# Twelve instead of eight K tiles of the mLSTM's gates and values in seven products

## The chip, the cores and the metric

The kernel runs on one core of one Trainium2 chip. It is a program for TensorE (matrix products), VectorE (DVE), ScalarE (ACT), GpSimd (POOL) and SyncE (SP, which issues most of the loads). The metric is the time of one execution on the device in microseconds (us); the kernel before takes 2147.57 us, the median of three runs (2147.09 to 2148.02).

## The reference

Two layers of an encoder trunk on x of shape (1, 256, 2048), all in float32. Layer 0 mixes with pooling and grouped-query attention, layer 1 with a bidirectional mLSTM of 8 heads of 256 dimensions; each layer ends with a gated MLP of width 5632. The change lies in the mLSTM of layer 1, which is, cut to what matters:

```
proj = h @ w_in                       # 256 x 2048 by 2048 x (4*2048 + 32)
q, k, v = proj's first three blocks of 2048 columns, by heads; q *= 256 ** -0.5
o_gate  = sigmoid(proj's fourth block of 2048 columns)
gates   = proj's last 32 columns + b_gate        # input and forget gates, both directions
w       = exp(log weights from the gates, running-max stabilised, causal or anti-causal)
scores  = (q . k) * w
h_t     = (scores @ v) / max(|sum of scores|, exp(-m))    # forward, and backward on the flipped sequence
y       = rms_norm per head(h_fw + h_bw) * o_gate;   x = x + y @ w_out
```

## The kernel before, in words

All matrix products take float32 operands as a high and a low part (the tiles `hl` for weights, index 0 high, index 1 low), and every product is three matmuls: high by high, high by low, low by high. Activations stand transposed: `norm.xx[:, k]` is K tile k (128 of the 2048 channels) for 256 tokens.

**Weights.** They arrive as a stream of chunks of 128 x 1024 numbers (512 KB), in the order in which TensorE uses them. `Stream.load` (L117) issues a chunk's load on SP's queue into one of seven raw buffers `w`; `Stream.split` makes the high part on ACT (L137) and the low part on DVE (L138) into one of four buffers `hl`. A chunk that is a sum of others is prepared in one of two ways. As `Made` it is summed beforehand in DRAM by `premix` (L491): ACT's queue copies a part into a scratch `m`, and POOL's queue adds other parts to it with accumulating DMAs, each of them held until a chosen matmul has run ("paced"). As `Chain` the raw part is loaded, and DVE adds the sum that stands in the preceding chunk (L133 and L134, two additions of 128 x 512) ahead of the split.

**TensorE's order** is written out by hand. The main products call `wv.tick`, and a weave (`Weave`) of generators puts the small matmuls of the heads (`qk`, `atr`, `av`, `htr`) between them: a generator yields the number of us of main products to wait before its next step. The orders of ACT, DVE, POOL and SP are made by a planner from the dependencies and its own durations.

**The mLSTM layer** (L780) first makes values and the 32 gate columns for heads 0 and 1 (`mv`), and `gates` turns the gate columns into rows: `gr` goes to DRAM as `gd`, and each head reads two rows of it back, broadcast over 128 partitions, into `G` (L874). It then goes over four pairs of heads `hp`. For each head `stat_group` makes q and k (`mq`, `mk`, 16 K tiles each), `scaled` gathers them, multiplies by the tokens' norm factor (q also by 256 ** -0.5, L854) and splits them into `hl_q`, `hl_k`; `head` is added to the weave. For the first three pairs `gates_values` follows (tiles `mp`, `mo`, `mv`): the output gate's 512 columns of this pair, and the values' 512 columns of the next pair, in one pass over K.

**Seven products.** Over K tiles 0 to 7, that is four pairs of K tiles (`ML_PAIRS`), this pass takes two token blocks by two K tiles by two column blocks with seven products instead of eight. `ML_ORDER` is its order: an `A` takes four products of a pair from two chunks (summed weights, `Made` or `Chain`) and sums of activations (`comb`, made by `combine`), a `B` two products from one chunk, a `P` one product each of two pairs from one chunk. The other K tiles are taken directly: a `D` (gates) or an `E` (values) is four products of two K tiles from one chunk. `first` and `second` combine the partial sums from PSUM on ACT and DVE into `og` and `vf`.

## Time and profile before

| | us |
|---|---|
| median of the runs (lowest, highest) | 2147.57 (2147.09, 2148.02) |
| the profiled execution's own time | 2147.11 |
| its span | 2145.3 |
| busy: TensorE, weight load, DVE, ACT, POOL | 2139.5, 1834.6, 1784.1, 1444.6, 287.6 |
| mLSTM from its first product to the output projection | 965.1 to 1344 |
| `gates_values` of the three pairs | 1038.1 to 1084.3, 1133.2 to 1177.4, 1226.2 to 1271.4 |

The times of the trace count from the start of the span; PE is TensorE's matmuls, PEld its weight loads. A group of instructions is given as line, engine, operation, tile out<-in, count, busy time, mean of one in ns, and the idle time of the engine ahead of it with what ended that. A window is given as us, then busy time (and count) of PE, PEld, DVE, ACT and POOL, the granted TensorE clock, the busy share of the DMA engines and GB/s.

### The profile page before, as it was taken

How to read it: one execution, taken by the hardware profiler on the slowest of the kernel's cores; microseconds unless marked ns; L12 is line 12 of the kernel's file. 1: busy time of each engine (PE TensorE's matmuls, PEld its weight loads, DVE VectorE, ACT ScalarE, POOL GpSimd, SP SyncE). 2: the span in 40 equal slices, each digit the busy share in tenths (PEclk: the TensorE clock that was granted, in tenths of full speed). 3: DMA queues.
4: the chain of work that ended last, by engine and by line, in shares of the span. 5: the costliest groups of instructions: out<-in, count | busy, mean ns of one | idle time of the engine just before them, and what ended most of it. 6: DMA issues, size and time to landing. Idle time of an engine off the chain costs nothing.

```text
span 2145.3 us, 32359 instructions
## 1 busy us (share of the span) xinstructions
PE 2139.5 (100%) x11364; PEld 1834.6 (86%) x11364; DVE 1784.1 (83%) x2524; ACT 1444.6 (67%) x2199; POOL 287.6 (13%) x366
## 2 busy tenths in 40 slices
PE   9999999999999999999999999999999999999999
PEld 7888888888888888889888888888888888888887
DVE  7786678889988899898878786567888899889988
ACT  6665577777777767766556564557776777777774
POOL 0022112111111111111111111111111111100000
PEclk9999999999999999999999999999999999999999
DMA  9678889899999999998889798988999999888875
GB/s 333 210 213 256 262 248 317 275 327 329 318 331 320 321 300 306 307 296 237 276 276 299 232 308 236 280 242 247 313 291 333 337 311 317 288 259 266 255 249 189
DMA packets 181543, 606.66 MB, mean 283 GB/s; under 512 B 23707, under 2 KB 26563, under 8 KB 181379
## 3 DMA queue, kind: packets, MB, share of 16 engines
q1 hardware_dynamic: 133952, 478.60, 62.4%
q0 software_dynamic: 28384, 70.54, 19.4%
q10 hardware_dynamic: 19042, 55.45, 7.8%
q8 instruction: 89, 1.46, 0.3%
q14 instruction: 76, 0.61, 0.1%
HBM read 602.35 MB, written 104.90 MB: 330 GB/s over the span
## 4 chain that ended last, share of the span: by engine, by line
PE 97%; DVE 2%; issue 1%; DMA 0%; ACT 0%; ACTq 0%; DVEq 0%
PE up L275 45%; PE pp L275 16%; PE op L275 8%; PE mq L275 4%; PE mk L275 4%; PE mo L275 3%; PE mv L275 3%; PE qproj L275 3%; PE dn L275 3%; PE mp L275 1%; PE kproj L275 1%; PE vproj L275 1%; DVE hl L138 1%; PE pool L275 1%; PE av L275 1%
## 5 line engine op out<-in xcount | busy, mean ns | idle before, releaser
L138 DVE TENSOR_TENSOR hl<-w,hl 128x1024 fp32r<-128x1024 f32 (+1 forms) x869 | 1048.0, 1217 | 179.1 <-ACT hl L137 172.1
L137 ACT CAST hl<-w 128x1024 fp32r<-128x1024 f32 (+1 forms) x868 | 891.2, 1046 | 384.8 <-PE up L275 118.3
L275 PE MATMUL up<-xx,hl 128*128 128x512 f32 (+1 forms) x5632 | 993.6, 337 | 0.0
L275 PEld LDWEIGHTS up<-xx,hl 128*128 128x128 f32 x5632 | 867.0, 188 | 130.0
L491 POOL DMA_DIRECT2D m<-m x184 | 147.4, 816 | 942.9 <-PE up L275 414.0
L275 PE MATMUL pp<-hl,s 128*128 128x512 f32 x912 | 226.5, 390 | 0.4
L275 PEld LDWEIGHTS pp<-hl,s 128*128 128x128 f32 x912 | 168.1, 188 | 34.4 <-DVE hl L138 1.6
L275 PE MATMUL pp<-hl,g 128*128 128x512 f32 x684 | 173.9, 390 | 0.0
L275 PEld LDWEIGHTS pp<-hl,g 128*128 128x128 f32 x684 | 125.8, 188 | 24.4
L441 ACT COPY tb_up<-up 128x512 f32<-128x512 f32 x88 | 51.6, 587 | 116.5 <-PE up L275 116.5
L1122 DVE TENSOR_TENSOR y<-y,z 128x510 f32<-128x510 f32 x88 | 60.8, 690 | 63.2 <-ACT y L1121 62.7
L1121 ACT ACTIVATE y<-tb_up,conv 128x256 f32<-128x256 f32 x176 | 103.7, 589 | 0.0
L491 POOL DMA_DIRECT2D m<-in_dn x80 | 69.2, 864 | 247.1 <-PE up L275 59.4
L275 PE MATMUL mk<-xx,hl 128*128 128x512 f32 (+1 forms) x512 | 93.0, 338 | 0.0
L275 PE MATMUL mq<-xx,hl 128*128 128x512 f32 (+1 forms) x512 | 92.0, 337 | 0.0
L442 DVE TENSOR_TENSOR tb_up<-up,tb_up 128x512 f32<-128x512 f32 x88 | 60.9, 692 | 36.9 <-ACT tb_up L441 36.5
L275 PE MATMUL op<-hl,cat 128*128 128x512 f32 x384 | 91.5, 393 | 0.0
L1119 ACT ACTIVATE z<-tb_up,conv 128x256 f32<-128x256 f32 x176 | 88.2, 501 | 3.9 <-DVE tb_up L1114 2.0
L275 PE MATMUL op<-hl,mcat 128*128 128x512 f32 x384 | 89.7, 392 | 0.0
L275 PEld LDWEIGHTS mq<-xx,hl 128*128 128x128 f32 x512 | 79.2, 188 | 11.6
L275 PEld LDWEIGHTS mk<-xx,hl 128*128 128x128 f32 x512 | 79.3, 188 | 11.4
L1120 ACT ACTIVATE z<-tb_up,conv 128x256 f32<-128x256 f32 x176 | 87.4, 496 | 0.0
(256 smaller groups left out, 2178.8 us busy)
## 6 DMA issues: line engine op xcount, KB each, us to landing
w<-in_up SPq DMA_DIRECT2D x352, 512.0 KB, 6.6
w<-in_dn SPq DMA_DIRECT2D x174, 512.0 KB, 6.0
w<-in_m_in SPq DMA_DIRECT2D x118, 512.0 KB, 6.0
w<-m SPq DMA_DIRECT2D x98, 512.0 KB, 5.7
m<-in_dn ACTq DMA_DIRECT2D x160, 256.0 KB, 5.8
m<-m POOLq DMA_DIRECT2D x184, 128.0 KB, 6.0
w<-in_a_in SPq DMA_DIRECT2D x45, 512.0 KB, 5.5
m<-in_dn POOLq DMA_DIRECT2D x80, 256.0 KB, 7.2
```

Source lines behind the costliest of these rows:

```text
L137: (self.nc.vector.tensor_copy if i + c == 0 else self.nc.scalar.copy)(hl[:, 0, c : c + n], w[:, c : c + n])
L138: low = self.nc.vector.tensor_sub(hl[:, 1, c : c + n], w[:, c : c + n], hl[:, 0, c : c + n].bitcast(F32))
L275: last_mm[0] = pe.matmul(out_, lhsT, rhs, start=start, stop=stop, skip_group_check=True)
L441: a.copy(tb, ps[:, :, 1, :])
L442: v.tensor_add(tb, ps[:, :, 0, :], tb)
L491: paced(eng.dma_start(to[p : p + P // 2], src[p : p + P // 2], **kw))
L1119: a.activation(z[:, 0, j, :], u[:, j, :], AF.Copy, scale=cw(tl, 0))
L1120: a.activation(z[:, 1, j, :], u[:, j, :], AF.Copy, scale=cw(tl, 2))
L1121: a.activation(y[:, j, :], u[:, j, :], AF.Identity, scale=cw(tl, 1), bias=cw(tl, 3))
L1122: v.tensor_add(y[:, :, 1:S], y[:, :, 1:S], z[:, 0, :, 0 : S - 1])
```

## The change

1. `ML_PAIRS` goes from 4 to 6: K tiles 0 to 11 are taken by seven products, K tiles 12 to 15 directly. `ML_ORDER` becomes six A, two D, six B, two E and three P, with A4, A5 and B0 to B5 in a row, where before a D stood behind each A. The activations' sums of pairs 4 and 5 get a tile of their own in the layer's constants.
2. In the third pass (`hp == 2`) each pair's second A chunk is a `Chain`; in the others, as before, only that of odd pairs.
3. q is no longer multiplied in `scaled`; its norm factor and 256 ** -0.5 stand in `qrcol`, one number for each token, and go into the operation that multiplies the scores by their weights (L891) in place of a 1.0. `hl_q` has one buffer in place of two.
4. `G` of head 0 is loaded from POOL's queue; the other heads' from ACT's.
5. The gaps of `head`: 14.0 and 9.0 for 10.0 and 6.0 ahead of `atr`, 5.0 for 3.2 ahead of `av`.
6. The premix of layer 1's MLP begins after the second pass instead of the first, one sum each 28.0 instead of 30.0; that of the mLSTM begins two up-projections later in layer 0's MLP, one sum each 18.0 instead of 25.0, and makes 18 sums instead of 12.

```diff
-ML_PAIRS = 4
-ML_ORDER = [(e[0], int(e[1:] or 0)) for e in "A0 D A1 D A2 D A3 D B0 B1 B2 E B3 E P0 E P2 E".split()]
+ML_PAIRS = 6
+ML_ORDER = [(e[0], int(e[1:] or 0)) for e in "A0 A1 D A2 A3 D A4 A5 B0 B1 B2 B3 B4 B5 E P0 P2 E P4".split()]
...
-            comb = actp.tile([P, ML_PAIRS, 2, 4, P], F32R, tag="B1", name="mcomb")
+            combs = [actp.tile([P, 4, 2, 4, P], F32R, tag="B1", name="mcomb0")]
+            combs.append(kp.tile([P, ML_PAIRS - 4, 2, 4, P], F32R, tag="mcomb", name="mcomb1"))
...
-            def scaled(ps, name, scale):
+            def scaled(ps, name):
                 u = gather(tp, ps, name)
-                v.scalar_tensor_tensor(u, u, scale, bc(norm.R, 2), ALU.mult, ALU.mult)
-                r = tp.tile([P, 2, 2, S], F32R, tag=name[0] + "hl", name=f"hl_{name}")
+                if name[0] == "k":
+                    v.tensor_mul(u, u, bc(norm.R, 2))
+                r = tp.tile([P, 2, 2, S], F32R, tag=name[0] + "hl", bufs=2 - (name[0] == "q"), name=f"hl_{name}")
...
-                    a.dma_start(G[:, d, :], gd[r : r + 1, :].to_broadcast([P, S]))
+                    (g if h == 0 else a).dma_start(G[:, d, :], gd[r : r + 1, :].to_broadcast([P, S]))
...
-                    v.scalar_tensor_tensor(arg[:, o : o + n], qk[:, t, c : c + n], 1.0, arg[:, o : o + n],
+                    v.scalar_tensor_tensor(arg[:, o : o + n], qk[:, t, c : c + n], qrcol[:, t : t + 1], arg[:, o : o + n],
...
-                yield 10.0 if h % 2 else 6.0
+                yield 14.0 if h % 2 else 9.0
...
-                yield 3.2
+                yield 5.0
...
+                    qrcol = kp.tile([P, 2], F32, tag="qrcol", name="qrcol")
+                    v.tensor_scalar_mul(qrcol, norm.rcol, MD ** -0.5)
...
-                hp == 0 and premix(1, 30.0, 30.0, 0)
+                hp == 1 and premix(1, 28.0, 28.0, 0)
...
-                    if layer == 0 and (c, i) == (len(FCH) - 2, 5):
-                        premix(2, 25.0, 25.0, 0)
+                    if layer == 0 and (c, i) == (len(FCH) - 2, 7):
+                        premix(2, 18.0, 18.0, 0)
...
-            made = [Made()] if j % 2 else [Made(), Made()]
+            made = [Made()] if j % 2 or hp == 2 else [Made(), Made()]
             part = [p[hp * ML_PAIRS + j] for p in parts]
             mixes.append(part + [made])
-            out += made + [Chain(part[2])] * (j % 2)
+            out += made + [Chain(part[2])] * (2 - len(made))
```

More of the change, by code (lines that the diff above doesn't have):

```diff
@@ L961, in combine @@
                 v.tensor_sub(sf[:, 3], g4[:, 2], sf[:, 2])
-                a.copy(comb[:, j, 0], sf)
-                v.tensor_sub(comb[:, j, 1], sf, comb[:, j, 0].bitcast(F32))
+                a.copy(comb(j)[:, 0], sf)
+                v.tensor_sub(comb(j)[:, 1], sf, comb(j)[:, 0].bitcast(F32))
             def combos():
@@ L1028, in gates_values @@
                     if kind == "A":
-                        xs = [[comb[:, j][:, i, m] for i in range(2)] for m in (1, 0, 2)] + [x_part(2 * j + 1, 1)]
+                        xs = [[comb(j)[:, i, m] for i in range(2)] for m in (1, 0, 2)] + [x_part(2 * j + 1, 1)]
                     elif kind == "B":
@@ L1032, in gates_values @@
                     elif kind == "P":
-                        xs = [[comb[:, j + k][:, i, 3] for i in range(2)] for k in range(2)]
+                        xs = [[comb(j + k)[:, i, 3] for i in range(2)] for k in range(2)]
                     else:
@@ L1072, in mlstm_layer @@
                     v.tensor_scalar_mul(hrcol, norm.rcol, 0.5)
+                    qrcol = kp.tile([P, 2], F32, tag="qrcol", name="qrcol")
+                    v.tensor_scalar_mul(qrcol, norm.rcol, MD ** -0.5)
                 for hh in range(2):
                     h = 2 * hp + hh
[L1075 to L1076 removed]
+                    q = scaled(stat_group(xx, list(range(KT)), f"mq{h}"), f"q{h}")
+                    kk = scaled(stat_group(xx, list(range(KT)), f"mk{h}"), f"k{h}")
                     wv.add(head(h, q, kk, vt, hh))
```

4 lines of the change are left out of this document (2 added, 2 removed).

## The prediction

> **What bounds the kernel now.** I read the page first, then the chain of waits for the whole span, then who waits for whom.
>
> ```profile
> span 2145.3 us, 32359 instructions
> PE 2139.5 (100%) x11364; PEld 1834.6 (86%) x11364; DVE 1784.1 (83%) x2524; ACT 1444.6 (67%) x2199; POOL 287.6 (13%) x366
> ...
> PE 97%; DVE 2%; issue 1%; DMA 0%; ACT 0%; ACTq 0%; DVEq 0%
> ...
> PE mo L275 <- DVE tb_k L442: 0.7, 1, 0.7
> PE atr L907 <- DVE A L901: 0.3, 1, 0.3
> ```
>
> TensorE works without a break; in the mLSTM it waits twice, 0.7 and 0.3 us. So a matmul taken out is worth its own pace, as long as DVE (83% busy) still delivers split weights. Its pace is read from the chain in order of time (start, us, count), with the borders of the second pass of gates and values:
>
> ```profile
> 1073.45 10.88 PE mv L275 x48
> ...
> 1115.89 1.43 PE qk L275 x12
> ...
> 1124.31 0.44 PE atr L907 x4
> ...
> 1128.24 1.43 PE av L275 x12
> ...
> 1133.15 2.05 PE mp L275 x9
> ...
> 1177.37 5.57 PE mq L275 x32
> ```
>
> 48 matmuls in 10.88 us are 0.227 us each, 0.68 us for a product of three. The windows show who has room in that pass (1133.15 to its last B at 1162.4, then to its end), beside two dense stretches of layer 0's MLP:
>
> ```profile
> 965.10:1344.00 378.90, 377.88 (x2108) 328.95 (x2107) 303.52 (x513) 223.51 (x302) 50.11 (x64) 1.00 0.87 266
> 1133.15:1162.40 29.25, 29.25 (x143) 24.64 (x143) 26.72 (x47) 19.77 (x26) 3.08 (x4) 1.00 0.87 287
> 1162.40:1177.40 15.00, 15.00 (x68) 12.43 (x67) 13.28 (x17) 9.84 (x12) 1.64 (x2) 1.00 1.00 342
> 1038.10:1069.40 31.30, 30.96 (x156) 26.12 (x155) 27.30 (x52) 20.72 (x30) 4.58 (x6) 1.00 0.90 276
> 1069.40:1084.30 14.90, 14.90 (x67) 12.33 (x67) 12.67 (x17) 9.61 (x12) 2.38 (x3) 1.00 0.99 339
> 901.00:925.00 24.00, 23.89 (x122) 20.03 (x122) 22.07 (x28) 17.61 (x26) 2.94 (x4) 1.00 0.97 318
> 701.00:780.00 79.00, 79.00 (x425) 67.92 (x424) 72.41 (x97) 56.68 (x86) 13.59 (x17) 1.00 1.00 315
> ```
>
> DVE is 26.72 of 29.25 us busy (91%) in the first part. In the MLP it was 22.07 of 24 (92%) while TensorE lost 0.11 us, and 72.41 of 79 while it lost nothing: DVE at 92% still feeds TensorE. The profiled execution took 2147.11 us, its span 2145.3, so 1.8 lie around it; the median of the runs is 0.46 above.
>
> **Costs, part by part.**
>
> ```profile
> L138 DVE TENSOR_TENSOR hl<-w,hl 128x1024 fp32r<-128x1024 f32 x145 | 176.9, 1222 | 47.3 <-ACT hl L137 45.9 <-DMA w<-in_m_in 0.3
> L133 DVE TENSOR_TENSOR w<-w,w 128x512 f32<-128x512 f32 x6 | 4.1, 686 | 0.4 <-DMA w<-in_m_s 0.4
> L134 DVE TENSOR_TENSOR w<-w 128x512 f32<-128x512 f32 x6 | 4.1, 686 | 0.0
> L854 DVE SCALAR_TENSOR_TENSOR tb_q<-tb_q,R 128x512 f32<-128x512 f32 x8 | 5.5, 688 | 0.1
> L956 DVE TENSOR_TENSOR mf<-xx 128x512 f32<-128x512 f32 x4 | 2.6, 663 | 0.0
> L959 DVE TENSOR_TENSOR msf<-mf 128x256 f32<-128x256 f32 x4 | 1.7, 413 | 0.0
> L960 DVE TENSOR_TENSOR msf<-msf,mf 128x128 f32<-128x128 f32 x4 | 1.1, 277 | 0.0
> L961 DVE TENSOR_TENSOR msf<-mf,msf 128x128 f32<-128x128 f32 x4 | 1.1, 285 | 0.0
> L963 DVE TENSOR_TENSOR mcomb<-msf,mcomb 128x512 fp32r<-128x512 f32 x4 | 2.7, 683 | 0.0
> L891 DVE SCALAR_TENSOR_TENSOR arg<-qk,arg 128x128 f32<-128x128 f32 x16 | 4.6, 286 | 0.4 <-PE qk L275 0.4
> L899 DVE SCALAR_TENSOR_TENSOR A<-arg,denr,A 128x128 f32<-128x128 f32 x8 | 2.8, 346 | 0.0
> ...
> 1152.54 2.35 DVE L138 TENSOR_TENSOR hl<-w,hl 128x1024 fp32r<-128x1024 f32 x2
> ...
> 1171.56 1.28 DVE L1022 TENSOR_TENSOR mvf<-mvf,mp 128x512 f32<-128x512 f32 x2
> ...
> L138 DVE TENSOR_TENSOR hl<-w,hl 128x1024 fp32r<-128x1024 f32 x15 | 18.2, 1222 | 1.5 <-ACT hl L137 1.2
> ...
> L137 ACT CAST hl<-w 128x1024 fp32r<-128x1024 f32 (+1 forms) x868 | 891.2, 1046 | 384.8 <-PE up L275 118.3
> ```
>
> *TensorE.* Each added pair needs seven products for eight: two pairs in three passes save 6 products, 6 x 0.68 = 4.1 us. That is all the change can gain beyond the two waits.
>
> A sentence of the Trainium skill ("Perfetto Trace Analysis", Identifying the Most-Contended Engine) bears on the price: matmul busy time flatters, weight-load busy time is the better measure. By it, with the 86% of PEld, an estimate of the gain is 3.5 us and the sum comes out at -2.9 instead of -3.5; the row's pace is elapsed time, so it decides.
>
> *Weights on DVE and ACT.* A pass takes 25 chunks instead of 22: two more pairs cost four A, two B and a P and save two D and two E. That is 9 more splits, 9 x 1.222 = 11.0 us of DVE and 9 x 1.05 = 9.4 of ACT, which idles 155 of 379 us. Chains go from 6 to 12: 6 x (0.686 + 0.686) = 8.2, and 0.4 if their raw parts are as late as those of the row (splits queue behind that wait). Two more `combine` are 2 x (0.663 + 0.413 + 0.277 + 0.285 + 0.683) = 4.6. Leaving q unscaled saves 8 x 0.688 = 5.5. The scores' factor from a tile may cost what L899 (0.346) has over L891 (0.286): 0 to 0.06 x 32 = 1.9; I take 1.9. DVE gets 20.2 us more in a stage of 379 us where it idles 379 - 303.5 = 75. As a sum this is covered; the danger is where it falls.
>
> *The dense stretch.* From A0 to the last B there are now 44 products, 29.9 us, with av of the even head (moved in by the gap 9.0), qk, atr and av of the odd head: 29.9 + 3 x 1.43 + 0.44 = 34.6 us of TensorE. Back to back splits follow at 2.35 - 1.22 = 1.13 us, additions at 0.60. Before, 15 splits (the row with x15; 17.0 us) left 26.7 - 17.0 = 9.7 us of other DVE work. Now 20 splits make 22.6, the other work 9.7, one more chain 1.2 and the scores' factor 0.2: 33.7 us of 34.6, or 97%. In the third pass A2 and A4 are chains too: 36.1 us, 104%. Against that stand the split weights that lie ahead: four buffers `hl` allow three chunks ahead, and two of them may be used up, 2.3 us. If DVE is busy all the time, no pass stalls (36.1 - 2.3 = 33.8). At the 92% of the row above, the first two need 33.7 / 0.92 - 2.3 = 34.3 and don't stall, the third 36.1 / 0.92 - 2.3 = 36.9 and stalls 2.3 us. Bounds 0 and 2.3; I take 1.2, the middle, since neither row is nearer. After the last B come E and q chunks with four products each, where DVE catches up; `second` is off the path.
>
> *Gaps.* `atr` of the odd head comes 4 us of products later, so the wait of 0.3 us goes. The wait of 0.7 for the gathered k falls at the third pass's start; `av` of the even head now runs after it, so its two ACT passes no longer stand before the gathering. It may stay or go: -0.7 to 0; I take -0.3. At the end, `htr` of head 7 comes some 35 us after mk7 (2.5 + 4.5 + 14 + 5 + 6 and a step's rounding each), and its rows are used after mo's 96 and op's first 144 matmuls, 54 us: hidden.
>
> *One buffer for hl_q.* The copy for head h+1 waits for qk of head h, which runs 7 us into the next q group of 10.3, so ahead of it. Only qk of head 0 (gap 6.0 + 4.5) comes some 1.3 us later than q's end; the ACT copy then holds up the splits behind it for up to 1.3 + 1.43 us, against three split q or k chunks ahead, of 2.8 us each (16 matmuls: 5.57 / 2): 0, at most 1. `mcomb1` moves the layer's tiles by 4 to 8 KB, so first writes may wait for other tiles of the MLP: 0, at most 1.
>
> *G of head 0 on POOL.*
>
> ```profile
> 998.57 0.36 ACTq L874 DMA_DIRECT2D G<-gd  x1
> 998.96 1.28 ACT L833 ACT_TABLE_LOAD   x1 [2.07 <-DMA gd<-gr]
> ...
> 990.17 0.59 POOL L361 DMA_DIRECT2D R<-rr  x1 [6.06 <-DMA rr<-re_n]
> ...
> 1007.07 0.85 ACT L880 ACTIVATE arg<-arg 128x768 f32<-128x768 f32 x1 [2.56 <-DVE arg L878]
> ```
>
> ACT loses a wait of 2.07 us, in which TensorE lost nothing; POOL takes it, with two issues of about 0.6 us by the row of R. Queued behind are paced premix transfers, due tens of us later. If G lands 2 or 3 us later, ACT waits longer at the exponential (2.56 now), and the splits behind it too, again within the 8.4 us of the three chunks: 0, bounds -0.5 and 1.
>
> *Premixes.*
>
> ```profile
> L491 ACTq DMA_DIRECT2D m<-in_m_s x36: 497/498/2508, 783.7 to 1102.0; - x36
> L491 POOL DMA_DIRECT2D m<-in_m_s x24: 772/778/824, 821.3 to 1138.2; - x24
> ...
> 762.17 11.14 PE up L275 x64
> ```
>
> Two up-projections with their units (24 matmuls, 5.4 us) are 33 us: the call comes at 784 - 25 + 33 = 792, the first of the 18 sums at 810, the last at 810 + 17 x 18 = 1116, and its transfers end 43 us later, over 80 ahead of their use. Six more single sums of four transfers are 12 issues more on ACT (6.0 us) and 12 on POOL (9.3), over 350 us: hidden. A double and a single sum move six times 0.52 MB, in 36 us instead of 50: 87 GB/s for 63, so 342 where the MLP's end now has 318. What is late first there are raw weights, and ACT's casts wait for them; seven raw buffers stand against that: 0, bounds 0 and 2. The next MLP's premix is lifted from the second pass, where TensorE doesn't wait: nothing comes of it; at 28 a sum instead of 30 it ends some 45 us later, against sums used one by one up to the MLP's end.
>
> Sum: -4.1 - 0.3 - 0.3 + 1.2 = -3.5. The profiled execution would take 2143.6, the median 2144.1.
>
> **Rivals.** *Everything is fed*: no stall and both waits gone, -5.1, 2142.5. For it: DVE's 72.41 of 79 at no loss; against: 104% in the third pass.
>
> *DVE becomes the bound* (the other side): the planner puts head work ahead of splits, the lead is used up before the dense run, and DVE works at 92%. Then the passes need 36.6, 36.6 and 39.2 against 34.6: 2.0 + 2.0 + 4.6 - 4.1 = +4.5, 2152.1. For it: 97% and 104%; against: the stretch at 901 ran without D chunks and lost 0.11. It decides from about 96%: there 0.5 + 0.5 + 3.0 eats the 4.1.
>
> *Weights come late.* The first pass moves 276 x 31.3 + 339 x 14.9 = 13.7 MB now; three chunks more make 15.3 in 44.5 us, 344 GB/s. If the 315 of the 79 us window is the limit, 48.6 us are needed and 4.1 lost: 2147.6, the gain gone. For it: the DMA engines' share is 1.00 there; against: 339 and 342 GB/s for 15 us with TensorE full. The Trainium skill ("DMA: Bandwidth & Descriptors", Where 436 GB/s comes from) has about 358 GB/s bind between HBM and SBUF; by that, an estimate for 15.3 MB is 42.7 us, and nothing is lost.
>
> **How the numbers follow.** The forecast (with the third pass's stall from 0 to 2.3 and the 0.7 gone or not, -4.4 to -2.1) has 0.50, everything fed 0.17, weights late 0.13 and DVE the bound 0.20. A change of 0.2%, 4.3 us, is about what a measurement of this kernel can tell from none: faster is below 2143.3, slower above 2151.9. Faster takes everything fed and a little of the forecast, 0.22; slower half of DVE the bound and a bit for late weights in several places, 0.14; the rest, 0.64, is within. The range goes from 2142.3 (all fed) to 2151.5, within the DVE case; the likeliest case alone is 2143.2 to 2145.5, or 2147.5 with one of the bounds of the smaller edits.
>
> **What would show it.** Right: 18 matmuls fewer, 11364 to 11346; DVE some 20 us busier, near 1804; the passes at some 44.3 us each (34.6 and 9.5), waits of TensorE for `hl` in the third pass only and below 2.5 us; no wait of `atr`. Wrong: waits of TensorE for `hl` (L138) in all three passes, or raw weights `w` as what ACT waits for between 850 and 960 or from 1038 to 1084, or ACT held at head 0's `arg` with TensorE idle behind it.

## The result and the profile after

The change makes the kernel a little slower. All ratios below are of one kernel's runs to runs of the kernel before on the same chip in the same session, with a 95% interval.

| | before | after |
|---|---|---|
| median of the runs of that session, us | 2147.09 | 2150.61 |
| lowest to highest (21 runs each) | 2146.83 to 2148.02 | 2147.97 to 2154.21 |
| ratio | | 1.0014 [1.0009, 1.002] |
| the profiled execution, its span | 2147.11, 2145.3 | 2148.62, 2146.8 |

The forecast was 2144.1, 3.5 below the median of before; the change came out 3 to 3.5 above it. The spread matters as much as the median: the kernel after scatters by 6 us. Its profiled execution is one of the better ones, 1.5 us above the profiled execution of before, so the trace shows about half of what the medians differ by.

The profile page of the kernel after begins like this (busy time with share and instruction count; then the shares of the chain that ended last):

```profile
span 2146.8 us, 32444 instructions
...
PE 2138.3 (100%) x11346; PEld 1830.7 (85%) x11346; DVE 1797.9 (84%) x2548; ACT 1455.1 (68%) x2210; POOL 302.0 (14%) x380
...
PE 91%; DVE 4%; DMA 2%; issue 2%; ACT 1%; ACTq 0%; POOL 0%; DVEq 0%; POOLq 0%
```

TensorE has 18 matmuls fewer, as the change says, and is busy 1.2 us less. But it is no longer 97% of the chain: DVE and DMA have come into it, and DMA stood at 0% before. Who TensorE waits for (total, times, longest, in us):

```profile
PE mk L275 <- DVE hl L138: 1.8, 1, 1.8
...
PE av L275 <- DVE at L916: 0.6, 1, 0.6
PE mv L275 <- DVE rv_h L280: 0.5, 1, 0.5
PE dn L275 <- DVE x L451: 0.2, 1, 0.2
```

The waits for `atr` and for the gathered `tb_k` are gone in this execution. In their place stands a wait for split weights in the first group of keys, `mk` of head 0.

Where the time goes is seen by stages. The table has the time from a stage's first product to the next stage's, taken from the start times of the matmuls. Up to the last down-projection of layer 0 the executions before and after run within 0.1 us of each other. From 1272 to TensorE's last product the kernel after is 1.15 us behind; the rest of the 1.5 by which the spans differ falls behind the last store. So what TensorE lost lies between 938 and 1272.

| stage, us | before | after | after, without the sums' additions (run no_adds) |
|---|---|---|---|
| last down-projection of layer 0 (`dn`, from 938) | 27.07 | 27.52 | 27.08 |
| first values and gates (`mv`) | 25.38 | 25.37 | 25.38 |
| keys of head 0 (`mk`) | 11.16 | 13.26 | 11.16 |
| first pass of `gates_values` | 46.22 | 47.19 | 44.57 |
| second pass | 44.22 | 44.48 | 44.48 |
| third pass | 45.20 | 45.46 | 45.48 |

A stage that contains `av` of an even head is 1.46 us longer, and the group before it that much shorter, since the longer gap moved `av` into the second and the third pass (in the first it stood before, too); so 44.22 before and 44.48 after for the second pass is a gain of 1.2, not a loss. The last column is what the passes cost with all their weights and products, and it is what the prediction had in mind: 44.3 for the first two.

**The first loss, in the first key group.** Head 0's gate rows go through DRAM to `G`; DVE makes `arg` from it, ACT the exponential. From the time lines of the kernel after (start, duration, and in brackets how long the engine stood idle ahead of it and for whom):

```profile
1003.05 1.14 POOL L880 DMA_DIRECT2D G<-gd  x2 [7.23 <-DMA gd<-gr]
...
1008.88 0.35 DVE L884 SCALAR_TENSOR_TENSOR arg<-G,mc,kml 128x128 f32<-128x128 f32 x1 [3.17 <-DMA G<-gd]
1010.82 1.14 DVE L884 SCALAR_TENSOR_TENSOR arg<-G,mc,kml 128x256 f32<-128x256 f32 x3 [1.59 <-DMA G<-gd]
...
1012.00 0.84 ACT L886 ACTIVATE arg<-arg 128x768 f32<-128x768 f32 x1 [7.12 <-DVE arg L884]
...
1013.96 2.60 PE L275 MATMUL mk<-xx,hl 128*128 128x256 f32 x14 [1.82 <-DVE hl L138]
```

Read downwards: `gd` and `G` are late, DVE stands for them in its order, ACT stands 7.12 us at the exponential (2.56 before), the casts of weights behind it are not done, and TensorE runs out of split weights.

**The second loss, in the first pass.** The chain of waits in order of time has these pieces of DMA among its longest (start, duration; `gd` and `G` belong to the first loss):

```profile
934.17 12.73 DMA w<-in_dn
...
996.67 5.84 DMA gd<-gr
...
1003.61 7.12 DMA G<-gd
...
1024.09 7.68 DMA w<-in_m_s
...
1050.24 7.56 DMA w<-in_m_s
...
1066.42 11.05 DMA w<-in_m_in
```

Of the others, the last two are raw weights in the first pass. ACT stands there for raw weights, 6.6 us in seven waits of the kernel after (1038 to 1088) and 1.1 us in the same window of run no_adds:

```profile
ACT hl L137 <- DMA w<-in_m_in: 6.6, 7, 2.1
...
ACT hl L137 <- DMA w<-in_m_in: 1.1, 2, 0.9
```

TensorE's weight loads then wait for split weights, a wait that the same view of no_adds does not list:

```profile
PEld mp L275 <- DVE hl L138: 1.3, 3, 0.5
PEld mv L275 <- DVE hl L138: 1.1, 2, 0.6
```

From 1038 to 1088 a load of 512 KB takes 10.0 us from issue to landing in the kernel after, by the list of its transfers:

```profile
w<-in_m_in SPq DMA_DIRECT2D x20, 512.0 KB, 10.0
```

and 6.9 in the kernel before:

```profile
w<-in_m_in SPq DMA_DIRECT2D x22, 512.0 KB, 6.9
```

### The profile page after: what moved, and what is told of

It is laid out like the page before. It is cut to its first block, busy times and chain, and to the rows that moved or that the text cites. A ratio compares the mean times of both kernels' runs of the same rounds, so it can differ in the third digit from the quotient of the medians.

```text
span 2146.8 us, 32444 instructions
## 1 busy us (share of the span) xinstructions
PE 2138.3 (100%) x11346; PEld 1830.7 (85%) x11346; DVE 1797.9 (84%) x2548; ACT 1455.1 (68%) x2210; POOL 302.0 (14%) x380
## 3 DMA queue, kind: packets, MB, share of 16 engines
q8 instruction: 89, 1.46, 0.3%
## 4 chain that ended last, share of the span: by engine, by line
PE 91%; DVE 4%; DMA 2%; issue 2%; ACT 1%; ACTq 0%; POOL 0%; DVEq 0%; POOLq 0%
PE up L275 45%; PE pp L275 16%; PE op L275 8%; PE mk L275 3%; PE mq L275 3%; PE qproj L275 3%; DVE hl L138 2%; PE mo L275 2%; PE mv L275 2%; PE dn L275 2%; PE mp L275 1%; PE kproj L275 1%; PE vproj L275 1%; DMA w<-in_m_s 1%; PE pool L275 1%
## 5 line engine op out<-in xcount | busy, mean ns | idle before, releaser
L137 ACT CAST hl<-w 128x1024 fp32r<-128x1024 f32 (+1 forms) x877 | 901.1, 1047 | 377.7 <-PE up L275 119.4
```

Of the source, the lines that this page charges most:

```text
L137: (self.nc.vector.tensor_copy if i + c == 0 else self.nc.scalar.copy)(hl[:, 0, c : c + n], w[:, c : c + n])
```

## The experiments

All runs, with the median, the range, and the ratio to the kernel before of the same session:

| run | us | ratio |
|---|---|---|
| again (the change, unaltered) | 2150.08 (2148.39 to 2153.35) | 1.0013 [1.0004, 1.0021] |
| g0_act | 2152.32 (2148.84 to 2154.12) | 1.0019 [1.001, 1.0027] |
| no_chain | 2147.75 (2145.61 to 2150.81) | 1.0 [0.9991, 1.0009] |
| no_premix | 2143.43 (2143.13 to 2143.87) | 0.9978 [0.9969, 0.9987] |
| no_adds | 2143.52 (2143.19 to 2143.78) | 0.9981 [0.9972, 0.999] |
| unread | 2151.54 (2150.57 to 2155.36) | 1.002 [1.0011, 1.0029] |
| plain_adds | 2147.76 (2146.77 to 2149.72) | 1.0002 [0.9993, 1.0011] |
| before_no_adds | 2147.31 (2146.99 to 2147.8) | 0.9999 [0.999, 1.0008] |
| before_dense | 2152.28 (2150.18 to 2157.7) | 1.0023 [1.0014, 1.0032] |
| pace22 | 2152.64 (2149.14 to 2155.3) | 1.002 [1.0011, 1.0029] |
| all_chain | 2148.77 (2147.45 to 2150.45) | 1.0005 [0.9996, 1.0014] |
| hold_g | 2152.16 (2150.05 to 2154.22) | 1.0019 [1.001, 1.0028] |
| hold_p | 2151.32 (2150.05 to 2153.08) | 1.0014 [1.0005, 1.0023] |
| paused | 2149.07 (2147.53 to 2150.36) | 1.0004 [0.9996, 1.0013] |
| four_first | 2148.94 (2147.64 to 2151.31) | 1.0007 [0.9998, 1.0016] |
| four_first22 | 2148.55 (2146.09 to 2151.09) | 1.0003 [0.9994, 1.0011] |
| four_hold | 2149.26 (2146.78 to 2151.0) | 1.0006 [0.9997, 1.0015] |
| rest_alone | 2153.11 (2150.19 to 2157.98) | 1.0028 [1.0017, 1.0038] |

### Size of the effect, GpSimd's part, DVE's part

The change run again, unaltered:

> The changed kernel once more, as the yardstick of the three runs beside it and for a second trace. Its first trace has TensorE stalled some 0.5 us in the last part of layer 0's MLP, 2.1 us in the first head's k group, 2.7 us in the first pass of gates and values and 0.9 in the third. If the late transfers cause most of it, the stalls differ from execution to execution, and the median lies again 2 to 4 us above the kernel before with runs from 1 to 7 above; if VectorE's load causes it, the stalls and times repeat within 0.5 us.

It came out at 1.0013, so the loss is real. In its profiled execution (2151.07) the first key group took 13.10 us, the first pass 47.70, the last down-projection 28.49: the same places, the last two worse.

Head 0's `G` back on ACT's queue:

```diff
-                    (g if h == 0 else a).dma_start(G[:, d, :], ...)
+                    a.dma_start(G[:, d, :], ...)
```

> The changed kernel with head 0's two rows of G issued on ACT's queue again, everything else as changed. Theory of the queue (ACT stands at head 0's exponential until G lands, and the splits behind it): the stall of 2.1 us in the first k group goes and the median falls by about 2 us, to 1 us above the kernel before. Theory of the transfers: G only comes as late on the other queue; the median falls by less than 0.7 us.

2152.32, where neither theory had the time rise, and the first key group took 14.79; ACT, which now sends `G` itself, stood 3.5 us idle when it sent it and 4.9 us at the exponential. That GpSimd begins head 0's rows is not what makes them late. The second pass took 46.65 in this execution, 2.2 more than in the change; the cause of that was not sought.

The 24 additions of the twelve chains left out (the chunk's raw part is split as it is):

```diff
-            out += made + [Chain(part[2])] * (2 - len(made))
+            out += made + [Chain(part[2], True)] * (2 - len(made))   # loaded, not added
```

> The changed kernel without the 24 chain additions of the mLSTM on VectorE (12 chunks, 2 of 0.69 us each); the chunks are split as they come, all transfers stay. Leaves those sums out. Theory of VectorE: with 97% and 104% of the dense stretches now 90% and 90%, the stalls of the passes go (3.6 us) and the time comes to 0 to 1 us above the kernel before. Theory of the transfers: the first pass still waits for raw weights; the median falls by less than 1 us.

2147.75, 2.3 below the run again and 0.3 above the kernel before: by its median what the theory of VectorE had said. By stages it is not. The third pass fell from 45.46 to 44.48, the first from 47.19 to 45.21; the first key group stayed long (13.83). So DVE's additions cost 1 us in the third pass and make the first pass more sensitive, but with 24 x 0.687 = 16 us of work taken from DVE the kernel still stands 4.3 us above the 2143.4 of the next run.

### The sums made in DRAM

The mLSTM's premix left out, all its copies and additions; a `Made` chunk loads one of its parts:

```diff
+        if layer == 2:
+            for s0, s1, r, made in mixes[2]:
+                for e, src in zip(made, (s0, r)):
+                    e.ap = src
+            return
```

> The changed kernel without the premix of the mLSTM: the summed chunks are replaced by one of their parts, loaded as it is, so the same number of weight loads, splits, chain additions and matmuls, but none of the 144 transfers that make the sums. Leaves the sums of the weights out. Theory of the transfers: the stalls in the MLP's end and in the first pass go (3.2 us) and the first k group's shrinks; 1 to 3 us below the kernel before, with runs within 1 us of each other. Theory of VectorE: the first pass keeps its 2.7 us; 2 to 3 us above the kernel before.

2143.43, a us lower than the theory of the transfers had it. Every loss but that of the third pass is gone, and so is the scatter: 0.7 us from lowest to highest.

Either the chunks wait for their sums, or the transfers get in the way of others. So the premix was run in full, and its sums not read:

```diff
-                e.ap = m[:, j]
+                e.ap = (s0, r)[j] if layer == 2 else m[:, j]
```

> The changed kernel with the mLSTM's premix running as changed, but its sums are not read: the chunks load one of their parts as it is, so no load waits for a sum. Leaves the sums of the weights out. Theory of contention (the premix's transfers slow the loads of weights and gate rows on the same DMA engines): still 2 to 4 us above the kernel before, with stalls in the first k group and the first pass. Theory of the dependency (loads in SP's queue wait for sums that are not ready, and the loads behind them too): as without the premix, 4 us below the kernel before.

2151.54, as slow as the change, though no load depends on a sum: the transfers themselves are in the way. The loss lay elsewhere in its profiled execution (first key group 16.21, first pass 45.37, second 46.92). In the kernel after, the loads' queue waits for no transfer into `m` between 930 and 1275, so its first pass didn't wait for sums either. Next, only POOL's accumulating transfers were left out, and ACT's copies kept:

```diff
-                    paced(eng.dma_start(to[p : p + P // 2], src[p : p + P // 2], **kw))
+                    if layer < 2 or not kw:
+                        paced(eng.dma_start(to[p : p + P // 2], src[p : p + P // 2], **kw))
```

> The changed kernel with the mLSTM's premix reduced to the copies on ACT's queue; the 96 accumulating transfers on POOL's queue are left out, and so are the sums. If the accumulating transfers are what slows the loads (POOL's queue held 22% of the DMA engines' time at the MLP's end for half the bytes of ACT's 12%), the stalls go: 3 to 4 us below the kernel before. If bytes alone count, half the excess stays: 0.5 us below to 1 above.

2143.52: it is these alone. There are 60 of them, and 48 copies; the two expectations that speak of 96 and 144 transfers count too many. The bytes in the expectation of this run are off, too: from 900 to 960 POOL's queue had 22.4% for 2.36 MB, ACT's 12.1% for 2.80 MB. Here a load of weights in the first pass lands after 6.1 us:

```profile
w<-in_m_in SPq DMA_DIRECT2D x24, 512.0 KB, 6.1
```

and the exponential of head 0 waits 4.26 us (7.12 with the additions), without TensorE noticing:

```profile
1008.70 0.85 ACT L887 ACTIVATE arg<-arg 128x768 f32<-128x768 f32 x1 [4.26 <-DVE arg L885]
```

Is it the adding, or only that bytes are moved by that queue? The same transfers as plain copies:

```diff
-                    paced(eng.dma_start(..., **kw))
+                    paced(eng.dma_start(..., **(kw if layer < 2 else {})))
```

> The changed kernel with the accumulating transfers of the mLSTM's premix made plain copies: same queue (POOL), same sizes and times of issue, no addition; leaves the sums out. If the read and addition at the destination make them costly, the stalls go: 3 to 4 us below the kernel before. If POOL's queue or the number of transfers does it, the time stays 2 to 4 us above.

2147.76, which neither theory had: the first pass is free (44.64), the first key group is not (14.91), and some 4 of the 7 us between 2143.5 and the change are there without any adding. The DMA queues bear on the first pass. POOL's queue is q0; the columns are packets, MB, and the share of the time of the 16 DMA engines. Kernel after, 1000 to 1040 and 1040 to 1090:

```profile
q0 software_dynamic: 804, 2.03, 31.3%
...
q0 software_dynamic: 794, 1.96, 21.2%
```

The same windows with plain copies:

```profile
q0 software_dynamic: 652, 1.96, 19.1%
...
q0 software_dynamic: 640, 1.97, 10.7%
```

The same bytes take 1.6 to 2 times the engines' time when they are added. (In the first window q0 carries `G` as well, 0.26 MB at 6.6% in run no_adds; with that taken off both, it is 1.9 times there.) In the first pass that is 10 points of the engines' time that the loads of weights lack.

The same transfers left out of the kernel before:

> The kernel before without the accumulating transfers of its mLSTM premix (48 on POOL's queue for 12 sums), copies on ACT's queue kept; leaves the sums out. Its trace has only 1.0 us of TensorE waits, so if these transfers cost it nothing, it stays within 0.5 us of the kernel before, at most 1 below; if they slow it in a way that its trace hides, it gains 2 to 4 as the changed kernel did.

2147.31, ratio 0.9999: there they cost the median nothing. (The slower runs may be another matter: the kernel before ran up to 2149.12 in that session and to 2150.97 in others, these ten runs to 2147.8.) And the kernel before, with the pace and the place of the call of the kernel after and nothing else of the change:

```diff
-                    if layer == 0 and (c, i) == (len(FCH) - 2, 5):
-                        premix(2, 25.0, 25.0, 0)
+                    if layer == 0 and (c, i) == (len(FCH) - 2, 7):
+                        premix(2, 18.0, 18.0, 0)
```

> The kernel before with one part of the change alone: its mLSTM premix (12 sums) called two up-projections later, one sum begun every 18 us instead of every 25. Theory of contention by rate: the stalls of the MLP's end and the first k group come up here too, 1.5 to 3 us above the kernel before. If the added chunks of the first pass or the other edits are needed for them, it stays within 0.5 us of the kernel before.

2152.28, 1.0023. The twelve sums of before, only denser and elsewhere, cost some 5 us by themselves. TensorE's wait in its profiled execution is again at head 0's gate rows, here directly; by stages all of the loss lies there (queries of head 0 16.59 instead of 12.35, keys 13.08 instead of 11.16), and the first pass, at 45.70, is no longer than before:

```profile
PE cols L275 <- ACT rows_b L833: 3.0, 1, 3.0
```

### Can the sums be put where they do no harm?

If density is the cause, sums spread further should cost less. Begun four up-projections earlier, one each 22 us:

```diff
-                    if layer == 0 and (c, i) == (len(FCH) - 2, 7):
-                        premix(2, 18.0, 18.0, 0)
+                    if layer == 0 and (c, i) == (len(FCH) - 2, 3):
+                        premix(2, 22.0, 22.0, 0)
```

> The changed kernel with the mLSTM's premix called four up-projections earlier and one sum begun every 22 us instead of every 18: the same 18 sums and transfers, 72 GB/s instead of 87. Theory of contention by rate: the stalls in the MLP's end and the first k group (0.5 and 2.1 us) shrink to under 1 in all, the first pass keeps part of its 2.7: 0 to 1.5 us below the kernel before. If only the number of transfers matters, it stays 2 to 4 us above.

2152.64, no better: the first pass took 51.74, the first key group 13.00. A miss for density as the only cause.

One sum and one chain for every pair in all passes, so that no pair has two sums to add up and DVE has more chains; begun two up-projections earlier, one each 21 us:

```diff
-            made = [Made()] if j % 2 or hp == 2 else [Made(), Made()]
+            made = [Made()]
```

> The changed kernel with every second A chunk of all three passes a Chain, so that all 18 sums need one accumulating addition each (9.4 MB of them instead of 12.6), and the mLSTM's premix called where it was before, one sum begun every 21 us: 25 GB/s of accumulating transfers, against 31 in the kernel before and 44 in the changed one. Theory of the accumulating transfers: no stall in the first k group and none for raw weights, but the first and second pass take VectorE's 0.9 us that the third pass has: about 2145.5, 2 us below the kernel before. If instead the extra chunks of the first pass are too much for the transfers at any pace, 1 to 3 us above.

2148.77, the same as before within the interval, and not the 2145.5 of the theory. The first key group is free (11.16), the first pass takes 48.00, the second 45.44. That DVE, with more chains, has less to spare when weights are late would fit; since the number of additions, the pace and the call changed with the chains, it isn't shown.

Then the pieces of the premix were held back at one place, by a flag that its generator looks at ahead of every piece. From the gate rows to head 0's `G`:

```diff
+                    while hold and layer == 2:
+                        yield 0.6
...
             def gates(ps):
+                hold.append(1)
...
                 yield 6.0 if h == 0 else 2.5
+                if h == 0:
+                    hold.clear()
```

> The changed kernel, complete, with the mLSTM's premix held back while the gate rows go to DRAM and head 0's G comes back (from the gates' generator to head 0's next step), then going on. Theory: the stall of the first k group is the chain of two small transfers, gd then G, that waits among the premix's; with none in flight G lands some 5 us sooner and 2 of the 2.1 us go. The first pass keeps its 2.7 us or more, since what was held comes later: 0 to 2 us above the kernel before. If G's lateness has another cause, 2.5 to 4 above.

And, with the same flag, from the first pass's first A to its last B:

> The changed kernel, complete, with the mLSTM's premix held back from the first pass's first A to its last B. Theory: the raw weights then come in time and the first pass takes 44.6 us instead of 47.2, the first k group keeps its 2.1: 0 to 1 us above the kernel before. If the pass is late for its own 25 loads, it keeps over 46 us.

These two tell the places apart. With `hold_g` the first key group is free (11.15) and the first pass takes 51.40; with `hold_p` the first pass is free (44.56) and the first key group takes 16.37, the second pass 46.72. Neither gains: 2152.16 and 2151.32, where at most 2 and 1 us above the kernel before were expected. The windows of the first pass, with the sums in it (hold_g; us, busy time and count of PE, PEld, DVE, ACT, POOL, clock, DMA share, GB/s):

```profile
1039.80:1091.20 51.40, 47.43 (x217) 37.83 (x216) 43.74 (x74) 33.33 (x47) 13.32 (x16) 0.97 1.01 317
```

and without (hold_p):

```profile
1044.50:1089.10 44.60, 44.60 (x217) 37.48 (x216) 43.20 (x71) 32.87 (x46) 4.69 (x5) 1.00 0.83 286
```

The same 217 records of matmuls, nearly the same work of DVE; 16 of POOL's instructions instead of 5, and the DMA engines full instead of at 0.83. What is held back in one place comes in a burst in the next.

Both holds at once, begun four up-projections earlier at 20 us a sum:

> Both holds, with the premix called four up-projections earlier and one sum begun every 20 us, so that all sums are still ready. If the two places are all that the premix costs, only the third pass's 0.9 us is left: 2.5 to 4 us below the kernel before, with runs within 1.5 us of each other. If the held transfers only move the stalls elsewhere, it stays above the kernel before.

2149.07, 1.0004: the held transfers move the stalls elsewhere. The first key group is free (11.16); the first pass takes 46.75, with a burst of held pieces behind its last B; and the earlier call costs elsewhere: TensorE waits 2.3 us for `hl` in layer 0's MLP.

### Four pairs in the first pass

The first pass needs four sums in the kernel before, six in the kernel after. So a mixture: the order of before with four pairs in the first pass, six pairs in the second and third, 16 sums at 24 us, near the old 25:

```diff
+ML_N = [4, 6, 6]
+ML_FOUR = [(e[0], int(e[1:] or 0)) for e in "A0 D A1 D A2 D A3 D B0 B1 B2 E B3 E P0 E P2 E".split()]
+ML_ORDERS = [ML_FOUR, ML_ORDER, ML_ORDER]
...
-                for kind, j in ML_ORDER:
+                for kind, j in ML_ORDERS[hp]:
...
-                    if layer == 0 and (c, i) == (len(FCH) - 2, 7):
-                        premix(2, 18.0, 18.0, 0)
+                    if layer == 0 and (c, i) == (len(FCH) - 2, 3):
+                        premix(2, 24.0, 24.0, 0)
```

> Seven products on four pairs of row tiles in the first pass (its order as before the change), on six pairs in the second and third: 16 sums in place of 18, and only six sums a pair of which are due by the second pass; the call stands at up (4,3) with a gap of 24, near the 25 of the kernel before. Four of the six products saved stay: -2.7. Theory (the density of the accumulating transfers around the first key group and the first pass costs the time): the first key group back at 11.2, the first pass at 46.2 as before the change, the third at 45.5 (its wait for VectorE's additions stays, +1): about 2145.3, 2144.5 to 2146.3, with a spread of some 1 us as before. Rival (the sums cost wherever the later chunks are mixed, also at this gap): the first key group or the first pass stay 1 to 3 us long, 2147 to 2149. Rival (the six pairs themselves, or GpSimd's gate rows, cost the time): the first key group at 13 or more with no sum beside it.

2148.94, not 2145.3. The passes are as expected (45.83, 44.48, 45.47), but the first key group took 12.88 at the old density: the exponential waits 6.72 us there.

> As the run with the gap of 24, with the call at up (4,5), where the kernel before has it, and a gap of 22: the last sum comes at the same time, the sums are a tenth denser and begin 31 us later. Theory (density): between the run with 24 and the change, 2145 to 2147.5, the loss if any in the first key group or the first pass. Rival (only the end of the sums matters): the same as the run with 24 within 0.5 us.

2148.55 (first key group 13.52, passes 46.91, 45.29, 45.48). The two can't be told apart by their medians, so this run decides nothing between density and the end of the sums.

With the pieces held at head 0's gate rows:

> As the run with four pairs in the first pass and the gap of 24, with no new piece of the premix sent off between the gate rows' round trip through memory and head 0's G. The four sums of the first pass are made before that, so none is missed in the first pass. Theory (the sums' presence beside the gate rows' small transfers stretches them, and beside the first pass's weights delays those): the first key group back at 11.2 from 12.9, the first pass at 46 to 47 if the pieces held come there: 2146.5 to 2148. Rival (the gate rows come late for another reason, GpSimd sending them or the heads' gaps): the first key group stays at 12.5 to 14, 2148.5 to 2149.5.

The first key group is back at 11.16, as the theory said; but the held pieces lengthen the first pass to 48.65, and in the profiled execution TensorE was 3.5 us late already at the end of layer 0's MLP: 2149.26, above the theory's range.

Last, the other parts of the change without the two pairs: four pairs in all passes, twelve sums at the old call and pace, against the kernel with four pairs in the first pass:

```diff
-ML_N = [4, 6, 6]
+ML_N = [4, 4, 4]
-ML_ORDERS = [ML_FOUR, ML_ORDER, ML_ORDER]
+ML_ORDERS = [ML_FOUR] * 3
...
-                hp == 1 and premix(1, 28.0, 28.0, 0)
+                hp == 0 and premix(1, 30.0, 30.0, 0)
...
-                    if layer == 0 and (c, i) == (len(FCH) - 2, 3):
-                        premix(2, 24.0, 24.0, 0)
+                    if layer == 0 and (c, i) == (len(FCH) - 2, 5):
+                        premix(2, 25.0, 25.0, 0)
...
-            made = [Made()] if j % 2 or hp == 2 else [Made(), Made()]
+            made = [Made()] if j % 2 else [Made(), Made()]
```

> The other parts of the change without its two added pairs: four pairs of row tiles in all passes, 12 sums at the call and gap of the kernel before, the third pass's chunks mixed as before; queries unscaled, the scale with the scores, head 0's G sent by GpSimd, the heads' longer gaps, the out-projection's premix where the kernel before has it. Theory (the sums alone cost the time): the first key group at 11.2, the passes as before, the waits for atr and tb_k gone: 2146.3 to 2147.3. Rival (GpSimd's part in the gate rows or the heads' gaps cost time by themselves): the first key group at 12.5 or more, 2148 to 2149.5.

2153.11, which neither expected. The first key group is free (11.15, with GpSimd sending `G`) and the first pass is as before (46.16): the theory's two places hold. The loss is in the second and third pass, 46.85 and 48.45. With the 1.46 us of `av` taken off, that is 1.2 and 1.8 more than before, the latter although the wait for `tb_k` is gone; and it is of another kind. Who TensorE waits for:

```profile
PE mv L278 <- DVE mvf L1023: 3.4, 2, 2.5
```

`mv`, the PSUM tile of the E chunks, takes the place of the tile that `first` reads, and `first`'s last subtraction comes late on DVE (second pass, time lines of DVE and PE):

```profile
1160.97 0.68 DVE L1023 TENSOR_TENSOR mvf<-mvf,mp 128x512 f32<-128x512 f32 x1
...
1161.80 2.33 PE L278 MATMUL mv<-hl,xx 128*128 128x512 f32 x9 [0.89 <-DVE mvf L1023]
```

In the old order the first E comes 10 products behind the last A (a D and three B); in the new one 12 (six B). The heads' longer gaps put `atr` and its `at` into just this stretch. So the gaps seem to belong to the new order and to cost time with the old one; no run changes them alone. The runs of this kernel lie up to 8 us above its profiled execution (2150.19, its lowest), and what the slower ones lose was not seen.

**Which pieces fall ahead of the gate rows.** The traces show one thing that separates the executions with a long first key group from the others. GpSimd's time line before `gd` is sent (996.67 in the kernel after):

```profile
993.55 0.57 POOL L361 DMA_DIRECT2D R<-rr  x1 [11.18 <-DMA rr<-re_n]
994.12 0.88 POOL L491 DMA_DIRECT2D m<-m  x1
994.67 1.14 POOL L491 DMA_DIRECT2D m<-in_m_s  x1
```

and in the kernel before (`gd` sent at 995.16):

```profile
996.28 0.80 POOL L491 DMA_DIRECT2D m<-m  x1 [5.52 <-PE mq L275]
```

In the kernel after, GpSimd stands for an earlier small round trip (`rr`, read back as `R`), and two pieces of the sums leave at once behind it, just ahead of `gd`. In the kernel before one piece leaves, 1.1 us behind `gd`. In all eleven profiled executions that lost time at the gate rows GpSimd sent two pieces in the 5.1 us ahead of `gd`, plain copies in plain_adds; in the nine others it sent at most one (one in all_chain, where `gd` landed after 4.14 us; none in the rest). So neither the pace nor the mere presence of sums separates them, but whether two pieces fall just ahead of this write. This is read from the traces, one execution of each kernel; no run moves these two pieces alone.

No complete kernel here beats the kernel before. The bound is 2143.5, for whoever makes the same chunks without these transfers of POOL's queue.

## Why the prediction was wrong

*The price of the products: right.* 11346 matmuls, and with the additions out of the way the profiled execution takes 2143.51 against 2147.11 of before, 3.6 less, where the sum said 3.5. That the two are so close is partly luck: the wait for `tb_k` went whole, 0.7 instead of the 0.3 taken, TensorE's last product ends 4.0 us sooner, and 0.4 of that is gone again behind it. But the elapsed pace of 0.68 us a product was the right one: key group and pass together, with the waits of 0.34 and 0.7 taken off, two products saved 1.4, 1.2 and 1.5 us in the three passes (the third without its chains, from no_chain), 4.1 in all. By the weight-load share, which the Trainium skill ("Perfetto Trace Analysis", Identifying the Most-Contended Engine) has as the better measure, the sum would have been -2.9.

*Weights on DVE: nearly.* The splits (878 for 869) and the chains (12 for 6) came as counted. The scores' factor from a tile cost what was taken:

```profile
L897 DVE SCALAR_TENSOR_TENSOR arg<-qk,qrcol,arg 128x128 f32<-128x128 f32 x16 | 5.5, 346 | 0.5 <-PE qk L275 0.5
```

346 ns where it had 286. DVE's busy time grew by 13.8 us instead of 20.2. I had summed durations; back to back, instructions overlap in the records (three splits in 3.49 us below, not 3.66), and that explains a part of it.

*The dense stretch: right in size by luck, wrong in kind.* I took 1.2 us for the third pass; it lost 1.0 (45.46 against 44.48 without the chains), and the first two nothing, once the sums are away. But TensorE doesn't wait for `hl` there. The kernel after at that place, DVE and then PE:

```profile
1258.50 3.49 DVE L138 TENSOR_TENSOR hl<-w,hl 128x1024 fp32r<-128x1024 f32 x3
1261.90 0.68 DVE L1020 TENSOR_TENSOR mvf<-mvf,mp 128x512 f32<-128x512 f32 x1
...
1262.73 2.98 PE L275 MATMUL mv<-hl,xx 128*128 128x512 f32 x12 [0.48 <-DVE rv_h L280]
```

It is `first`'s last subtraction that holds the PSUM tile of `mv`, late behind three splits. This is read from the times, for the row names the next small instruction on DVE; in rest_alone the row names the subtraction itself. I had looked at DVE as a supplier of weights only. It also frees PSUM, and in rest_alone TensorE waited for that 0.9 and 2.5 us.

*Gaps, one buffer for hl_q, mcomb1: right within their bounds.* The wait of `atr` is gone. That of `tb_k` is gone in the profiled execution and back, with 0.7, in that of the run again. No wait for `hl_q` shows.

*G of head 0 on POOL: the term was 0, bounds -0.5 and 1; the place lost 2.1.* The issuing engine is not the cause (g0_act, rest_alone). What failed is the sentence that two or three us more are "within the 8.4 us of the three chunks". Where ACT stood 2.6 to 4.3 us at the exponential TensorE lost nothing; where it stood 6.7 and 7.1, it lost 1.7 and 2.1. The lead was some 5 us in these two (7.12 - 2.1 and 6.72 - 1.7) and 3 in hold_p (8.24 - 5.2), not 8.4. It was also not so that the premix's transfers were "due tens of us later": in the kernel after GpSimd sent one 1.1 us behind `G`, and in the kernel before pieces left at 1000.46 and 1005.16. And the rows were later by more than I allowed: `gd` took 5.84 us to land instead of about 3.4.

*Premixes: the failed step.* I took 0, between 0 and 2, and it cost some 7 us by the medians (2150.61 or 2150.08 against 2143.5). Three errors stand in it. I priced the sums by their bytes (87 GB/s for 63) and held these against the GB/s of a stretch. The queues' rows were there to see in the profile of before (1040 to 1090, q1 the loads of weights, q0 the sums):

```profile
q1 hardware_dynamic: 3321, 12.12, 66.6%
q0 software_dynamic: 591, 1.49, 16.4%
```

16.4% for 1.49 MB is twice as much a byte as 66.6% for 12.12. I placed the danger at the MLP's end, where it was 0.5 us (1.4 in the run again), and not at the gate rows, whose small transfers have no buffers ahead of them. And I read "nothing is lost before" as room. before_dense shows that there was none: the sums of before lie where they cost nothing (before_no_adds), and moving them costs 5 us. Both places showed the signs that the prediction had named for being wrong: ACT waiting for raw weights between 1038 and 1084, and ACT held at head 0's `arg` with TensorE idle behind it.

The Trainium skill ("DMA: Bandwidth & Descriptors", Queues, rings and completion order) says that an engine goes round the queues that have work, a packet from each. This fits what is seen, small transfers slower beside other queues' packets, though no run here shows the order of packets.

*The rival "Weights come late": the place was right, the cause was not.* The first pass did stall for raw weights, and the bytes were as worked out: 15.3 MB forecast, and by this window of the kernel after 47.2 us at 323 GB/s, 15.2 MB.

```profile
1040.50:1087.70 47.20, 46.30 (x218) 37.05 (x217) 42.84 (x71) 32.86 (x47) 10.22 (x12) 1.00 0.98 323
```

But the three added chunks don't do it; without the additions the same chunks pass at 313 GB/s with TensorE full, in 44.57 us:

```profile
1038.00:1082.00 44.00, 44.00 (x214) 36.98 (x213) 42.30 (x70) 32.24 (x46) 2.25 (x2) 1.00 0.91 313
```

The GB/s don't tell the two apart, and neither does the engines' share alone, 0.98 against 0.91: the second pass of the kernel after lost nothing at 0.96.

```profile
1135.10:1179.50 44.40, 44.40 (x216) 37.30 (x215) 42.35 (x70) 32.38 (x44) 6.42 (x6) 1.00 0.96 321
```

What differs is when the loads land, after 10.0 us in the stalled pass, 7.7 in this one and 6.1 in no_adds. The figure of about 358 GB/s that the Trainium skill ("DMA: Bandwidth & Descriptors", Where 436 GB/s comes from) has bind, and by which I had nothing lost, did not decide: the stage stalled at 323 on average, and its last half, where it still lost time, ran at 358 (1064 to 1087.7, at a share of 1.03). Nor is the figure a limit here: no_adds moved 419 GB/s from 1064 to 1075 with TensorE full.

*DVE becomes the bound* did not happen, though the chains made the first pass more sensitive (45.21 without them).

**What stays open.** At the gate rows, that the sums' transfers cause the loss is shown by taking them out (no_adds) and by holding them back (hold_g, paused, four_hold); that it takes two pieces just ahead of `gd` is read from the traces and not tested. For the first pass, holding them back frees it (hold_p), and so do plain copies; why it took 51.74 at a slower pace (pace22) is not known. Why the runs of one kernel scatter by 4 to 8 us as soon as the sums overlap these places, and by 0.6 without them, was seen but not traced.

## What to carry to other kernels

Price a transfer by the share of the DMA engines' time that its queue has in the profile, not by its bytes; additions in DRAM took twice the time of loads a byte here. Before a background stream is made denser or moved, look at what it will run beside, and which of its pieces leave just ahead: small round trips through DRAM on the path (here gate rows, 3 to 5 us of lead) come first, then stages whose loads land late already. A high share of the engines' time is by itself no sign of loss (0.96 in the second pass). That a stream costs nothing where it lies is no evidence of room next to it; taking it out of both kernels (before_no_adds, no_adds) and moving it alone (before_dense) are the cheap tests.

## What the runs showed of the hardware that I had not expected

- An accumulating transfer from DRAM to DRAM took 1.6 to 2 times the DMA engines' time of a plain copy of the same bytes on the same queue (31.3% against 19.1% with `G` on the queue in both, 21.2% against 10.7%).
- Beside them, loads of 512 KB landed after 10.0 us instead of 6.1, and a write of 40 KB after 5.84 us instead of about 3.4.
- The scatter of a kernel's times went with the background transfers: 2143.19 to 2143.78 without the additions, 2147.97 to 2154.21 with them.
- In hold_g the granted clock in the first pass was 0.97, where TensorE worked 47.43 of 51.40 us, and 1.00 in every undisturbed pass; no run here tells which of the two causes the other.
